# One encoder layer on one core: linear attention's scores in two groups, gate logits and norm sums as high and low parts, two groups of attention values together, and a second queue for the first loads

## The chip, the core and the metric

The kernel runs on one core of a Trainium2 chip. Time is device microseconds of one execution, and the figure for a kernel is the median over several executions. Beside it stands one execution under the hardware profiler, whose span (first to last instruction) and rows are used for all the reasoning. The engines are named as in the profile: PE (matmul) and PEld (its weight loads, which overlap with PE), DVE (VectorE), ACT (ScalarE), POOL (GpSimd) and SP (SyncE, which mostly issues DMAs). ACT and POOL can issue DMAs too.

## The reference

One layer of a hybrid streaming encoder over 512 tokens of width 2048, all in float32. Cut to what matters here:

```python
h = rms_norm(x)
q_a, k_a, v_a, q_g, k_g, v_g, r_g, gate_lr = split(h @ w_in)
# group A: 16 heads of 64, softmax attention over a band of chunks, learned bias by distance
y_a = chunked_band_attention(q_a, k_a, v_a, bias)
# group B: 4 heads (key width 128, value width 256), chunks of 64 tokens
gate_logit = gate_lr @ w_gate_up + b_gate          # rank 16 -> 512
log_a = log_sigmoid(gate_logit) / 16
b = cumsum(log_a within a chunk)
attn = tril((q_g * exp(b)) @ (k_g * exp(-b)).T)    # within a chunk
o_g = attn @ v_g + (q_g * exp(b)) @ S              # S: state carried over the chunks
y_g = rms_norm(o_g, over 256) * silu(r_g)
x = x + concat(y_a, y_g) @ w_out
x = x + (gelu(conv3(up gate)) * conv3(up value)) @ w_ffn_down
x = x + sigmoid(rms_norm(x) @ w_ple_gate) * (p @ w_ple_proj)
return rms_norm(x)
```

## The kernel before

Activations are kept transposed: features on the 128 partitions, the 512 tokens along the free axis. The large products run in fp32r, the faster matmul type, with each fp32 operand split into a high part (a copy rounded to fp32r, made by ACT) and a low part (the difference, made by DVE), and three products high-high, high-low and low-high. `vproj` and `proj` do this for 128x512 tiles. Small products of linear and softmax attention run in plain fp32, which the profile shows as two PE passes each.

The program has three parts.

The start: eleven matmuls of a tile of ones (`pw`, L82) keep PE busy while the first loads travel. All loads go out on SP: the first half of the first value weight, `cols` (all the small per-feature vectors), the first block of `x`, the second half of the weight, and so on (`wtile`, `load_input`). ACT begins with a one-element activation, `warm`, which makes it load its function table.

Linear attention (from about 85 to 317 us in the profile): two value projections `vproj`; the low-rank gate `plr`, whose 32 rows hold the 16 outputs for the high and for the low half of the weight; then for each of four heads `gla_proj` (gate logits `pz` at L1077, exponentials, key and query projections `pk` and `pq`) and `gla_core`. `gla_core` transposes the keys (`pkt`), forms the scores `pat`, the state updates `pu`, the outputs `po`, the sum of squares `s2`, and hands it to `rstd_wide`, whose one fp32 matmul with a matrix of ones (`msw`) spreads the sum over all partitions. `pat` is made of two products for each of four 128-token tiles: a 128x128 one (L1139) and one with 64 output rows for the odd chunk against the even one (L1141). A head's core is issued behind the next head's projections, and two value projections for softmax attention (`values_a`) surround the last core. In this part the order on each engine comes from the scheduler of the tile framework.

The unit machine (from 317 us on): every remaining large product is a "unit" of seven products of 24 matmuls of 128x256 (a two-level block scheme: PLAIN gives their order P1, P2, P6, P5, P7, P3, P4). Units run one after the other as a list of steps, one product a step. From here on `keep_in_program_order` fixes each engine's order as written. Other work is hung on the steps by an agenda: an entry (step, k) runs its function before the product for k up to 1 and behind it for k over 1. The first two steps are `embedding` products `pp`; units 0 to 7 of the front stage are query/key projections, and `attend` hangs the softmax attention of two heads on the steps that follow each. It works in three groups h = 0, 1, 2 of query tiles (TILES): scores, `soft` (bias, maximum, exponential), `normal` (divide by the sum), `turn` (transposes `ptr`), `evict` (ACT copies `ptr` to `PT`) and `values` (`py`, fp32 with 64 output rows, the two heads in the two halves of the PSUM bank). Units 8 to 11 are the output gates of linear attention; then come the output projection `wo`, the feed-forward stages, and the embedding gate.

PSUM: linear attention uses four banks for accumulators (`mm`) and four for small results (`aux`). The unit machine reopens the eight banks as tags b0 to b7, which take their place in the order in which they are first used. Since the first user is `pp`, on the tags b5, b6, b7, b4, these get the banks that hold the last value projection.

Raw weights, high parts and low parts lie in rings of three pages each (`wr`, `wh`, `wl`) in the first two parts; a load into a page waits until the page's former content has been split.

The order of the items in a step, around the change:

```python
(5, 6, scores), (6, 1, soft), (7, 1, normal), (7, 5, turn), (8, 1, evict), (8, 4, values)   # each + h
```

Of the kernel before, what the change touches and what calls it, by code (L numbers as in the profile page):

```python
# [8 lines left out]
F32 = mybir.dt.float32  # L9
F32R = mybir.dt.float32r  # L10
I32 = mybir.dt.int32
AF = mybir.ActivationFunctionType
ALU = mybir.AluOpType

P = 128
# [26 lines left out]
def encoder_block(ctx: ExitStack, tc: tile.TileContext, A, out):  # L42
# [33 lines left out]
    epst = cp.tile([P, 1], F32, name="epst")  # L76
    nc.gpsimd.memset(epst, EPS)
    warm = cp.tile([P, 1], F32, name="warm")
    nc.scalar.activation(warm, ones[:, 0:1], AF.Copy)
    pw = pa.tile([P, T], F32, tag="aux", name="pw")  # L80
    for _ in range(11):
        nc.tensor.matmul(pw[:, :P], ones, ones, start=True, stop=True)  # L82
# [104 lines left out]
        ten.matmul(pb, ones, dg[:, :nt * P], start=True, stop=True)  # L187
        return pb

    def rstd_wide(sumsq, n, dst, a):  # L190
        c = sumsq.shape[1]
        ms = psum_aux("msw")[:, :c]
        ten.matmul(ms, ones, sumsq, start=True, stop=True)
        act.activation(dst, ms, AF.Ln, scale=1.0 / n, bias=epst)
        t = tp.tile([P, T], F32, tag="dg", name="nwt")[:, :c]
        vec.tensor_scalar(a, ms, 1.0 / n, EPS, ALU.mult, ALU.add)
        act.activation(dst, dst, AF.Exp, scale=-0.5)
        vec.tensor_tensor(t, dst, dst, ALU.mult)
        vec.scalar_tensor_tensor(t, t, -0.5, a, ALU.mult, ALU.mult)
        vec.scalar_tensor_tensor(dst, t, 1.5, dst, ALU.add, ALU.mult)  # L200
# [6 lines left out]
    def xslot(i, name):  # L207
        return pairs[i % 8][:, i // 8, :]
# [4 lines left out]
    gnw = cols[:, 4 * KD + 4:4 * KD + 6]  # L213

    h1 = []

    def load_input(kt):
        if kt == 0:
            nc.sync.dma_start(cols, A["cols"])
        xt = xslot(kt, f"x0_{kt}")  # L220
        nc.sync.dma_start(xt, A["x"][kt])
        h = slot(kt, f"h1_{kt}")
        split_scaled(h, xt, nmix[:, kt:kt + 1])
        h1.append(h)
        return xt
# [469 lines left out]
    def attend(unit):  # L695
# [42 lines left out]
                    ten.matmul(psc[:, w], ql, M["Kl", s][:, :nn], start=False, stop=True)  # L738

        def soft(h):  # L740
            t, at = tile_("sc", 1024, bufs=2), 0
            for s in range(2):
                for i, qt in enumerate(TILES[h]):
                    n = P * (qt + 1)
                    sc = M["sc", s, qt] = t[:, at:at + n]
                    mx = M["mx", s, qt] = tile_("mx", 4, bufs=8)
                    at += n
                    vec.tensor_tensor_reduce(sc, M["psc", s, h][:, 256 * i:256 * i + n], bias[:, s, T - n:T], 1.0, -3.0e38,
                                             ALU.add, ALU.max, mx[:, 0:1])
                    vec.tensor_scalar(mx[:, 1:2], mx[:, 0:1], -1.0, None, ALU.mult)  # L750
                    act.activation(sc, sc, AF.Exp, bias=mx[:, 1:2], accum_out=mx[:, 2:3])
# [14 lines left out]

        def evict(h):
            n = 3 * P if h else T
            M["PT"] = tile_("PT", 2 * T).rearrange("p (s t) -> p s t", s=2)
            for s in range(2):  # L770
                act.activation(M["PT"][:, s, :n], M["ptr", s][:, :n], AF.Copy)

        def values(h):
            if h == 0:
                M["y"] = pp_.tile([P, T], F32, tag="b3", name="py")
            for i, qt in enumerate(TILES[h]):
                for kt in range(qt + 1):
                    for s in range(2):
                        o = (2 * i + kt) * P
                        ten.matmul(M["y"][s * 64:(s + 1) * 64, qt * P:(qt + 1) * P], M["V"][:, kt, s * 64:(s + 1) * 64],  # L780
                                   M["PT"][:, s, o:o + P], start=kt == 0, stop=kt == qt)

        def result():
            if b % 2 == 0:
# [5 lines left out]
            items.append((12, 1, lambda: store_pair(mixd, b // 2, ypair[0][:, 0, :], ypair[0][:, 1, :])))  # L790
        for h in range(3):
            items += [(t + h, k, lambda f=f, h=h: f(h)) for t, k, f in (
                (5, 6, scores), (6, 1, soft), (7, 1, normal), (7, 5, turn), (8, 1, evict), (8, 4, values))]
        return items

    tails = [None, None]
# [229 lines left out]
    with ExitStack() as mix:  # L1026
        vp = mix.enter_context(tc.tile_pool(name="v", bufs=1, side="right"))

        with ExitStack() as gctx:
# [20 lines left out]

            for c in range(2):
                vproj(A["w_v_g"], c, lambda t: V[:, t, c * T:(c + 1) * T], c == 0, input_pair if c else None)
            up2 = gp.tile([P, T], F32, name="up2")[0:32]
            nc.sync.dma_start(up2, A["gate_up"])

            gl = page("wr", "wgate_r")
            nc.sync.dma_start(gl[:, :256], A["w_gate"])
# [7 lines left out]
            for kt in range(KD):  # L1065
                w = glh[:, kt * 32:kt * 32 + P]
                nc.tensor.matmul(plr, w, h1[kt][:, 0, :], start=kt == 0, stop=False)
                nc.tensor.matmul(plr, w, h1[kt][:, 1, :], start=False, stop=kt == KD - 1)
            lr = gp.tile([P, T], F32, name="lr")[0:32]
            nc.vector.tensor_tensor(lr, plr[0:32, :], rb[0:32, :], ALU.mult)  # L1070

            def gt(name, tag, bufs=1, cols=T):
                return gp.tile([P, cols], F32, tag=tag, name=name, bufs=bufs)
# [49 lines left out]
            def gla_core(hd, eb, en, dd, dec2):  # L1123
# [13 lines left out]
                for t in range(TT):  # L1137
                    sl = slice(t * P, (t + 1) * P)
                    nc.tensor.matmul(pat[:, sl], en[:, sl], eb[:, sl], start=True, stop=True)  # L1139
                    e0, o0 = t * P, t * P + CHUNK  # L1140
                    nc.tensor.matmul(pat[0:CHUNK, o0:o0 + CHUNK], dd[:, e0:e0 + CHUNK], eb[:, o0:o0 + CHUNK],  # L1141
                                     start=True, stop=True)
# [33 lines left out]
                        nc.vector.tensor_tensor(s2, s2, s3, ALU.add)  # L1176
                    o.append(ov)
                rg = gt("rg", "rg")
                rstd_wide(s2, 256, rg, gt("nwa", "nwa"))
                for vb in range(2):  # L1180
                    nc.vector.scalar_tensor_tensor(o[vb], o[vb], gnw[:, vb:vb + 1], rg, ALU.mult, ALU.mult)
                    nc.sync.dma_start(ond[hd][:, vb], o[vb])
# [40 lines left out]
    values_a(1, operand_step, operands_left)  # L1223
    pctx.close()
    pp_ = ctx.enter_context(tc.tile_pool(name="banks", bufs=1, space=PSUM, reuse_waits="tile"))
    aux[0] = aux_bank
    actx = ExitStack()

# [210 lines left out]
```

## Time and profile before

| what | value |
|---|---|
| time, median of 3 | 2319.01 us (2318.95 to 2320.66) |
| profiled execution | 2315.06 us |
| its span | 2313.4 us |
| mean granted PE clock | 0.995 |
| PE / DVE / ACT / POOL busy | 98% / 81% / 56% / 6% of the span |
| DMA | 516.64 MB, 223 GB/s on average |
| chain that ended last | PE 86%, DVE 6%, DMA 4%, ACT 2%, issue 2% |

In a row of the timeline stand start, duration, engine, line, operation, output and inputs, shapes, count, and in brackets the idle time of the engine just before with what ended it. A matmul's duration is its latency through the array; matmuls overlap, so what one costs is the distance from its start to the next one's start. Where a helper records an instruction, its line is L64.

### The profile page before, as it was taken

The page shows a single profiled execution, that of the slowest core. Times are in us where ns is not written, and L with a number is a line of the kernel's source. Part 1 is how long each engine was busy: PE and PEld are TensorE (multiplying, and loading weights), DVE is VectorE, ACT ScalarE, POOL GpSimd, SP SyncE. Part 2 cuts the span into 40 slices and gives each one's busy share as a digit, 9 for nine tenths or more (in the row PEclk, how much of TensorE's full clock was granted, in tenths as well). Part 3 has the DMA queues.
Part 4 walks back from the last instruction along what each step waited for, and adds up shares of the span by engine and source line. Part 5 has one row for each costly group of instructions (what it writes and reads, how often), then busy time and mean ns, then how long its engine had stood idle before and what let it go on. Part 6 is the DMA issues. An engine that isn't in the chain of part 4 may idle for free.

```text
span 2313.4 us, 44977 instructions
## 1 busy us (share of the span) xinstructions
PE 2272.6 (98%) x18020; PEld 2191.4 (95%) x18020; DVE 1885.2 (81%) x2584; ACT 1295.3 (56%) x1899; POOL 143.0 (6%) x180
## 2 busy tenths in 40 slices
PE   9999999999999999999999999999999999999996
PEld 8878889999989999999999999999999999999996
DVE  6556358888778888998888888888898787898986
ACT  6344356777555665555555555555564554656655
POOL 0000000000000000000000000000000100000000
PEclk9999999999999999999999999999999999999999
DMA  6622586666978977787877777777866967779894
GB/s 219 194 78 87 167 288 170 181 182 186 308 245 265 316 221 206 214 220 209 223 204 219 212 214 207 216 209 219 267 206 228 314 216 251 267 252 330 263 294 164
DMA packets 195473, 516.64 MB, mean 223 GB/s; under 512 B 20896, under 2 KB 72352, under 8 KB 195264
## 3 DMA queue, kind: packets, MB, share of 16 engines
q1 hardware_dynamic: 166272, 422.54, 52.1%
q0 software_dynamic: 23616, 84.95, 20.9%
q10 hardware_dynamic: 5376, 6.29, 0.8%
q8 instruction: 141, 2.31, 0.4%
q14 instruction: 68, 0.56, 0.1%
HBM read 435.05 MB, written 76.55 MB: 221 GB/s over the span
## 4 chain that ended last, share of the span: by engine, by line
PE 86%; DVE 6%; DMA 4%; ACT 2%; issue 2%; ACTq 0%; DVEq 0%; POOL 0%; SPq 0%; POOLq 0%
PE accA L64 39%; PE accC L64 21%; PE accB L64 10%; PE v L249 3%; PE v L250 2%; PE v L251 2%; DVE wl L64 1%; PE py L64 1%; PE psc L64 1%; PE ptr L64 1%; DVE s L64 1%; PE pk L133 1%; PE pk L132 1%; DMA wo_T<-mix_T 1%; PE pk L134 1%
## 5 line engine op out<-in xcount | busy, mean ns | idle before, releaser
L64 DVE TENSOR_TENSOR wl<-s,wh 128x1024 fp32r<-128x1024 f32 (+1 forms) x365 | 437.7, 1200 | 65.2 <-ACT wh L64 64.1
L64 ACT ACTIVATE wh<-l 128x1024 fp32r<-128x1024 f32 (+1 forms) x308 | 319.2, 1037 | 182.8 <-PE accC L64 120.3
L64 DVE TENSOR_TENSOR wl<-l,wh 128x1024 fp32r<-128x1024 f32 (+1 forms) x308 | 368.0, 1195 | 61.9 <-ACT wh L64 61.2
L64 ACT ACTIVATE wh<-s 128x1024 fp32r<-128x1024 f32 (+1 forms) x365 | 377.8, 1036 | 39.2 <-DVE s L64 20.4
L64 ACT ACTIVATE u<-accA 128x256 f32<-128x256 f32 x290 | 109.4, 377 | 363.4 <-PE accA L64 363.2
L64 DVE TENSOR_TENSOR s<-s,l 128x1024 f32<-128x1024 f32 (+1 forms) x192 | 229.6, 1196 | 11.0 <-DMA s<-in_w_blk 10.8
L64 PE MATMUL accA<-up_T,wh 128*128 128x256 f32 x1408 | 178.8, 279 | 0.1
L64 PEld LDWEIGHTS accA<-up_T,wh 128*128 128x128 f32 x1408 | 170.7, 188 | 0.3 <-ACT wh L64 0.3
L64 DVE SCALAR_TENSOR_TENSOR cv<-u,cw,cv 128x511 f32<-128x511 f32 (+1 forms) x176 | 131.6, 748 | 3.1
L404 POOL DMA_DIRECT2D s<-in_w_up x88 | 75.1, 853 | 788.6 <-DMA s<-in_w_up 366.2
L250 PE MATMUL v<-wv_l,h 128*128 128x512 f32 x256 | 100.5, 392 | 0.0
L249 PE MATMUL v<-wv_h,h 128*128 128x512 f32 x256 | 100.3, 392 | 0.0
L251 PE MATMUL v<-wv_h,h 128*128 128x512 f32 x256 | 99.9, 391 | 0.0
L64 PE MATMUL accA<-up_T,wl 128*128 128x256 f32 x704 | 96.4, 279 | 0.0
L64 PE MATMUL accA<-dn_T,wh 128*128 128x256 f32 x704 | 91.6, 282 | 4.5 <-ACT wh L64 4.5
L64 PE MATMUL accB<-up_R,wh 128*128 128x256 f32 x704 | 90.4, 280 | 2.0 <-DVE up_R L64 1.3
L64 PEld LDWEIGHTS accA<-dn_T,wh 128*128 128x128 f32 x704 | 86.8, 190 | 5.1 <-ACT wh L64 5.1
L64 ACT ACTIVATE u<-accC 128x256 f32<-128x256 f32 x94 | 35.9, 382 | 96.2 <-PE accC L64 96.1
L64 PE MATMUL accA<-up_R,wh 128*128 128x256 f32 x704 | 89.7, 280 | 0.0
L64 PE MATMUL accC<-up_R,wh 128*128 128x256 f32 x704 | 89.3, 279 | 0.0
L64 PE MATMUL accC<-up_N,wh 128*128 128x256 f32 x704 | 89.3, 279 | 0.0
L64 PE MATMUL accA<-up_N,wh 128*128 128x256 f32 x704 | 89.3, 279 | 0.0
(383 smaller groups left out, 5124.1 us busy)
## 6 DMA issues: line engine op xcount, KB each, us to landing
l<-in_w_up SPq DMA_DIRECT2D x132, 512.0 KB, 5.5
s<-in_w_up SPq DMA_DIRECT2D x88, 512.0 KB, 4.8
s<-in_w_up POOLq DMA_DIRECT2D x88, 512.0 KB, 6.1
l<-in_w_dn SPq DMA_DIRECT2D x56, 448.0 KB, 5.5
l<-in_w_blk SPq DMA_DIRECT2D x36, 512.0 KB, 4.4
l<-in_w_out SPq DMA_DIRECT2D x28, 512.0 KB, 5.1
l<-in_w_dn SPq DMA_DIRECT2D x28, 512.0 KB, 5.5
s<-in_w_blk SPq DMA_DIRECT2D x24, 512.0 KB, 4.3
```

What stands on the lines that cost most here:

```text
L64: ins = f(*args, **kw)
L132: nc.tensor.matmul(po, whi, act[:, 0, :], start=start, stop=False)
L133: nc.tensor.matmul(po, whi, act[:, 1, :], start=False, stop=False)
L134: nc.tensor.matmul(po, wlo, act[:, 0, :], start=False, stop=stop)
L249: nc.tensor.matmul(ps[t], h1[kt][:, 0, sl], wh, start=kt == 0, stop=False)
L250: nc.tensor.matmul(ps[t], h1[kt][:, 0, sl], wl, start=False, stop=False)
L251: nc.tensor.matmul(ps[t], h1[kt][:, 1, sl], wh, start=False, stop=kt == KD - 1)
L404: nc.gpsimd.dma_start(t, src("L22" if name == "S1" else "L11"), accum_op=ALU.add)
```

## The change

Seven edits.

1. First loads. `x[0]` and then `cols` are issued by ACT, ahead of its table load and `warm`, instead of by SP, so that SP issues the two halves of the first weight back to back.
2. Gate logits. `pz` becomes one fp32r matmul over 128 rows instead of an fp32 one over 32. The gate weight is loaded three times into one raw page and split (`up2`: high, high, low, zero), and the low-rank activations are split alike (`lr`: high, low, high, zero). For that `up_r` takes a page of the ring `wr`, `gate_up` is loaded by three DMAs in place of one, and there are new small operations: one POOL memset, four ACT copies, two DVE subtractions.
3. Norm sums. `s2` is split into `s2h` (ACT) and `s2l` (DVE), and `msw` becomes two fp32r matmuls with a copy of the ones (`ones_r`) instead of one fp32 matmul.
4. Scores of linear attention. The four 128x128 products of `pat` come first, then the four with 64 output rows.
5. Values of softmax attention. `values` of group 1 moves one step later, where `values` of group 2 runs: the twelve matmuls of each head pair stand together. `PT` grows from 1024 to 1536 columns to hold both groups.
6. `sc` becomes one buffer of 1024 columns (groups 0 and 2) and one, `scb`, of 768 (group 1), instead of two of 1024.
7. Four unused tiles are opened first on the tags b0 to b3, so that these take the four former accumulator banks, and b4 to b7 the four former `aux` banks.

The scheduler of the first two parts also shifts neighbours: the first `pz` stands some ten matmuls further down in PE's order, `msw` of each head three further down with its second half behind one more matmul, and in heads 2 and 3 `pz` between the two halves.

```diff
-    nc.scalar.activation(warm, ones[:, 0:1], AF.Copy)
...
-    def rstd_wide(sumsq, n, dst, a):
-        c = sumsq.shape[1]
+    def rstd_wide(ones_r, parts, n, dst, a):
+        c = parts[0].shape[1]
         ms = psum_aux("msw")[:, :c]
-        ten.matmul(ms, ones, sumsq, start=True, stop=True)
+        for i, q in enumerate(parts):
+            ten.matmul(ms, ones_r, q, start=i == 0, stop=i == len(parts) - 1)
...
+    first = xslot(0, "x0_0")
+    nc.scalar.dma_start(first, A["x"][0])
+    nc.scalar.dma_start(cols, A["cols"])
+    nc.scalar.activation(warm, ones[:, 0:1], AF.Copy)
     def load_input(kt):
-        if kt == 0:
-            nc.sync.dma_start(cols, A["cols"])
-        xt = xslot(kt, f"x0_{kt}")
-        nc.sync.dma_start(xt, A["x"][kt])
+        xt = xslot(kt, f"x0_{kt}") if kt else first
+        if kt:
+            nc.sync.dma_start(xt, A["x"][kt])
...
-            t, at = tile_("sc", 1024, bufs=2), 0
+            t, at = (tile_("scb", 768) if h == 1 else tile_("sc", 1024)), 0
...
-            M["PT"] = tile_("PT", 2 * T).rearrange("p (s t) -> p s t", s=2)
+            if h < 2:
+                M["PTt"] = tile_("PT", 3 * T)
+            pt = M["PT", h] = M["PTt"][:, 768 * (h == 2):][:, :2 * n].rearrange("p (s t) -> p s t", s=2)
...
-                (5, 6, scores), (6, 1, soft), (7, 1, normal), (7, 5, turn), (8, 1, evict), (8, 4, values))]
+                (5, 6, scores), (6, 1, soft), (7, 1, normal), (7, 5, turn), (8, 1, evict), (8 + (h == 1), 4, values))]
...
-            up2 = gp.tile([P, T], F32, name="up2")[0:32]
-            nc.sync.dma_start(up2, A["gate_up"])
+            upr = page("wr", "up_r")[:, :T]
+            nc.gpsimd.memset(upr[96:P], 0.0)
+            for i in range(3):
+                nc.sync.dma_start(upr[32 * i:32 * i + 32], A["gate_up"])
+            up2 = gp.tile([P, T], F32R, name="up2")
+            nc.scalar.activation(up2, upr, AF.Copy)
+            nc.vector.tensor_tensor(up2[64:96], upr[64:96], up2[64:96].bitcast(F32), ALU.subtract)
...
-            lr = gp.tile([P, T], F32, name="lr")[0:32]
-            nc.vector.tensor_tensor(lr, plr[0:32, :], rb[0:32, :], ALU.mult)
+            lr = gp.tile([P, T], F32R, name="lr")
+            lf = gp.tile([P, T], F32, tag="lf", name="lrf")[0:32]
+            nc.vector.tensor_tensor(lf, plr[0:32, :], rb[0:32, :], ALU.mult)
+            nc.scalar.activation(lr[0:32], lf, AF.Copy)
+            nc.scalar.activation(lr[64:96], lf, AF.Copy)
+            nc.scalar.activation(lr[96:P], attn_t[0][96:P], AF.Copy)
+            nc.vector.tensor_tensor(lr[32:64], lf, lr[0:32].bitcast(F32), ALU.subtract)
+            ones_r = gp.tile([P, P], F32R, name="ones_r")
+            nc.scalar.activation(ones_r, ones, AF.Copy)
...
                     nc.tensor.matmul(pat[:, sl], en[:, sl], eb[:, sl], start=True, stop=True)
+                for t in range(TT):
                     e0, o0 = t * P, t * P + CHUNK
...
-                rstd_wide(s2, 256, rg, gt("nwa", "nwa"))
+                sh, sl = (gp.tile([P, T], F32R, tag=n, name=n) for n in ("s2h", "s2l"))
+                nc.scalar.activation(sh, s2, AF.Copy)
+                nc.vector.tensor_tensor(sl, s2, sh.bitcast(F32), ALU.subtract)
+                rstd_wide(ones_r, (sh, sl), 256, rg, gt("nwa", "nwa"))
...
     pp_ = ctx.enter_context(tc.tile_pool(name="banks", bufs=1, space=PSUM, reuse_waits="tile"))
+    for t in range(4):
+        pp_.tile([P, T], F32, tag=f"b{t}", name="unused")
```

More of the change, by code (lines that the diff above doesn't have):

```diff
@@ L768, in evict @@
             n = 3 * P if h else T
-            M["PT"] = tile_("PT", 2 * T).rearrange("p (s t) -> p s t", s=2)
+            if h < 2:
+                M["PTt"] = tile_("PT", 3 * T)
+            pt = M["PT", h] = M["PTt"][:, 768 * (h == 2):][:, :2 * n].rearrange("p (s t) -> p s t", s=2)
             for s in range(2):
-                act.activation(M["PT"][:, s, :n], M["ptr", s][:, :n], AF.Copy)
+                act.activation(pt[:, s], M["ptr", s][:, :n], AF.Copy)
         def values(h):
@@ L780, in values @@
                         ten.matmul(M["y"][s * 64:(s + 1) * 64, qt * P:(qt + 1) * P], M["V"][:, kt, s * 64:(s + 1) * 64],
-                                   M["PT"][:, s, o:o + P], start=kt == 0, stop=kt == qt)
+                                   M["PT", h][:, s, o:o + P], start=kt == 0, stop=kt == qt)
         def result():
```

## The prediction

> **What bounds the kernel now.** I read the page first, then windows by stage, then the timeline of PE at every place that the diff touches, then the chain of waits over the passage from the query and key units to the output projection.
>
> ```profile
> PE 2272.6 (98%) x18020; PEld 2191.4 (95%) x18020; DVE 1885.2 (81%) x2584; ACT 1295.3 (56%) x1899; POOL 143.0 (6%) x180
> ...
> PE 86%; DVE 6%; DMA 4%; ACT 2%; issue 2%; ACTq 0%; DVEq 0%; POOL 0%; SPq 0%; POOLq 0%
> ```
>
> ```profile
> 100.00:317.00 217.00, 216.72 (x1014) 174.82 (x1012) 110.81 (x150) 93.80 (x111) 1.97 (x3) 1.00 0.41 131
> ...
> 330.00:553.00 223.00, 222.96 (x1954) 215.05 (x1952) 197.49 (x454) 155.70 (x307) 14.46 (x17) 1.00 0.67 188
> 553.00:620.00 67.00, 64.42 (x536) 61.58 (x535) 47.67 (x90) 38.28 (x60) 4.26 (x5) 0.97 0.82 244
> 620.00:680.00 60.00, 54.50 (x406) 50.94 (x405) 49.73 (x67) 40.49 (x65) 3.40 (x4) 1.00 0.91 297
> ```
>
> The windows give, after the stretch and its length, the busy time of PE, PEld, DVE, ACT and POOL, then PE's granted clock, the DMA engines' share and GB/s. In linear attention (100 to 317) PE is busy for 216.72 of 217 us and DVE for half; in the softmax attention (330 to 553) for 222.96 of 223, with DVE at 89%. So in both a PE slot that is saved brings the end of the stage forward by its length, and work added to ACT or DVE costs nothing while it comes in time. Behind 553 PE does wait, and DMA is busier.
>
> **1. First loads.** Rows of the timeline, weight loads of PE:
>
> ```profile
> 1.20 4.77 PEld L82 LDWEIGHTS pw<-ones 128*128 128x128 f32 x22 [1.20 <-POOL ones L75]
> 6.29 0.29 PEld L249 LDWEIGHTS v<-wv_h,h 128*128 128x128 f32 x1 [0.32 <-ACT h L154]
> ```
>
> The warm-up products keep their number, and their last weight load ends at 5.97; the first real one waits 0.32 us longer, for the first block of `x`. The change issues that block two queue entries earlier, so it should no longer be late, but PE can gain no more than the 0.32. SP's later loads go out earlier too. ACT's table load and `warm` move behind its two DMA issues, in time in which ACT waits for the weight anyway. Below zero: sharing the engines with the first weight half could make that later; I bound it by the same 0.32. I take 0.25 (0.32 to -0.32).
>
> **2 and 3. Gate logits and norm sums.** PE's rows; a cost is the distance between starts.
>
> ```profile
> 159.30 0.40 PE L132 MATMUL pk<-h,wkg_h 128*128 128x512 f32 x1
> 159.55 1.12 PE L64 MATMUL msw<-s,ones 128*128 128x512 f32 x2
> 160.61 1.12 PE L1077 MATMUL pz<-lr,up 32*128 32x512 f32 x2
> ...
> 162.00 0.39 PE L134 MATMUL pk<-h,wkg_l 128*128 128x512 f32 x1
> ```
>
> ```profile
> 222.59 0.40 PE L249 MATMUL v<-wv_h,h 128*128 128x512 f32 x1
> 222.84 1.12 PE L64 MATMUL msw<-s,ones 128*128 128x512 f32 x2
> ...
> 224.04 0.39 PE L251 MATMUL v<-wv_h,h 128*128 128x512 f32 x1
> 224.27 0.39 PE L249 MATMUL v<-wv_h,h 128*128 128x512 f32 x1
> ```
>
> An fp32r product of 128x512 costs 0.23 (224.04 to 224.27). From 222.59 to 224.04 lie two such products and `msw`: 1.45 - 0.46 = 0.99 for `msw`. From 159.30 to 162.00 lie two of them, `msw` and `pz`: 2.70 - 0.46 = 2.24, so `pz` costs 1.25. Four heads: 4 x 2.24 = 8.96. New: one product for `pz`, two for `msw`, 12 x 0.23 = 2.76. Gain 6.2.
>
> What could be late instead:
>
> ```profile
> 158.14 0.63 ACT L1175 ACTIVATE s<-pair_r 128x512 f32<-128x512 f32 x1 [0.71 <-DVE pair_r L1170]
> ```
>
> ```profile
> 158.81 0.69 DVE L1176 TENSOR_TENSOR s<-s,s 128x512 f32<-128x512 f32 x1
> ```
>
> The sum of squares is ready at 159.50. `s2h` on ACT (0.63, as the row of ACT) gives 160.13, `s2l` on DVE (0.69) 160.82. PE's new places are three products behind the old one (159.55 + 0.69 = 160.24), and for the second half two more (160.70). So the first is just in time and the second about 0.1 late. On ACT the logarithm of the norm waits behind `s2h` and the next gate's first activation; PE needs neither soon. I charge 0.1 per head, at worst 0.7 (a whole `s2l`). The first `pz` waits for a longer chain (product, two copies, subtraction), but stands ten products, 2.3 us, further down; that is about its length, so at most one copy, 0.63, is exposed; I take zero. Gain 6.2 - 0.4 = 5.8, between 6.2 and 2.8.
>
> The page for `up_r` and its three DMAs push the gate weight back:
>
> ```profile
> 88.66 0.42 ACT L1062 ACTIVATE glh<-wgate_r 128x256 fp32r<-128x256 f32 x1 [1.43 <-DMA wgate_r<-in_w_gate]
> ```
>
> ```profile
> L1067 PE MATMUL plr<-h,glh x16: 389/394/404, 95.4 to 102.4; 128*128 128x512 f32 x16
> ```
>
> Its split starts at 88.66, is 0.4 us of ACT and as much of DVE, and PE wants it at 95.4. Three issues ahead of it, `up2`'s copy (0.63) and subtraction (0.69) come to under 3 us; the slack is over 5. Nothing. The memset is on an idle POOL, `ones_r` and the zero rows lie in the first 40 us, where PE runs without a wait.
>
> **4. Scores.**
>
> ```profile
> 149.39 0.39 PE L1139 MATMUL pat<-eb,en 128*128 128x128 f32 x2
> 149.71 0.33 PE L1141 MATMUL pat<-eb,dd 128*64 128x64 f32 x2
> 149.97 0.49 PE L1139 MATMUL pat<-eb,en 128*128 128x128 f32 x2
> 150.39 0.33 PE L1141 MATMUL pat<-eb,dd 128*64 128x64 f32 x2
> ...
> 152.00 1.56 PE L1151 MATMUL pu<-Vg,kT 128*128 128x256 f32 x6
> ...
> 154.09 0.61 PE L1166 MATMUL po<-attnT,Vg 128*128 128x128 f32 x4
> 154.53 0.39 PE L1168 MATMUL po<-eb,S 128*128 128x128 f32 x2
> ```
>
> ```profile
> L1141 PEld LDWEIGHTS pat<-eb,dd x32: 132/134/136, 149.7 to 267.3; 128*64 128x64 f32 x32
> ```
>
> Today the eight products take 152.00 - 149.39 = 2.61. Fp32 products of one shape cost 0.22 (154.09 to 154.53 holds two); in `pat` the 128x128 ones cost 0.32 and 0.42, the small ones 0.26, so each change of shape adds 0.1 to 0.2. Grouped: three at 0.22, one at 0.32 before the change, three small ones, one small one at 0.26 before the next shape. If the three small ones cost half of a 128x128 one, 0.11 to 0.13, the sum is 1.6 and a head gains 1.0; if each still costs its 0.26, the sum is 2.02 and a head gains 0.6. I take the first, since half the columns stream: 4 x 1.0 = 3.9 with the roundings, between 4.1 and 2.4. The Trainium skill bears on this (TensorEngine Tiling (Array Packing), Tiling Modes and Restrictions and Gotchas): changing the tiling mode drains the engine, which agrees with the 0.1 to 0.2 above, but column tiling also switches the fast weight load off. The second speaks against my value; it is the third rival.
>
> **5 and 6. Values of two groups.**
>
> ```profile
> 406.13 1.09 PE L64 MATMUL py<-PT,va 128*64 128x128 f32 x16
> 407.16 0.87 PE L64 MATMUL ptr<-ident,sc 128*128 128x128 f32 x6
> ...
> 409.76 1.10 PE L64 MATMUL accA<-in_N,wl 128*128 128x256 f32 x8
> 410.79 0.88 PE L64 MATMUL py<-PT,va 128*64 128x128 f32 x12
> 411.60 0.88 PE L64 MATMUL ptr<-ident,sc 128*128 128x128 f32 x6
> ...
> 417.99 1.10 PE L64 MATMUL accA<-in_T,wl 128*128 128x256 f32 x8
> 418.92 2.03 PE L64 MATMUL accC<-in_R,wh 128*128 128x256 f32 x16
> ```
>
> Eight value products (16 passes) take 1.03, six 0.81: 0.11 each plus 0.15 fixed. Entering costs another 0.10 (409.76 to 410.79 is 1.03, the same eight matmuls before a product of their own shape 0.93). One visit fewer saves 0.25 a unit. The transposes of group 2 move up by 0.81, to the end of their step's product, about 3 us behind the step's start where DVE did the division; in units 0 to 6 PE does not wait there. In unit 7 it does:
>
> ```profile
> 579.52 0.63 PE L64 MATMUL ptr<-ident,sc 128*128 128x128 f32 x3 [0.22 <-DVE mx L64]
> ```
>
> There DVE is the bound, and what PE saves it waits. Seven units: 1.8, bounds 2.2 (unit 7 too) and 0 (each such wait eats the visit). The buffers `sc`, `scb` and `PT` are each rewritten at least as long after their last reader as now: nothing.
>
> **7. Banks.**
>
> ```profile
> 317.77 0.73 PE L64 MATMUL pp<-ps,wh 128*128 128x512 f32 x2 [1.05 <-ACT pair_c L255]
> ```
>
> The first `pp` waits for ACT to evict the last value projection. With `pp` in the former `aux` banks that wait goes, since its inputs were ready before. Late next is the fifth `pp`, which needs the first one's bank; PE comes there at about 322.2 and ACT has emptied it at about 321.9. Gain 1.05, at worst 0.
>
> **The sum.** 0.25 + 5.8 + 3.9 + 1.8 + 1.05 = 12.8, best 13.9, worst 4.9 with all lower ends at once. The profiled execution took 2315.06 us with a span of 2313.4, 4 us less than the median 2319.01. I carry the difference over: span 2300.6, profiled 2302.3, median 2306.
>
> **The rivals.**
>
> First, the passage to the output projection absorbs it. The chain of waits there:
>
> ```profile
> 584.53 10.39 DMA s<-in_w_blk
> ...
> 635.00 14.68 DMA wo_T<-mix_T
> ```
>
> DMA shares of 0.82 and 0.91 speak for it: if the data could not come sooner, PE would arrive 12 us earlier and wait that long. Against it: before, the share is 0.67 with no backlog, and both transfers are issued by work that itself moves up. Up to the point where these waits take all of it, 2319.
>
> Second, slower: the transfers there meet in another order. SP issues in order, so one entry that waits holds all behind it:
>
> ```profile
> SPq L273 <- DVE u L64: 9.2, 1, 9.2
> ```
>
> A gain of 12.8 and 4.6 beyond it are used up by two more holds of this length (18.4) in front of loads that PE needs: 2325. One alone leaves it faster, 2315. It decides from 17.4 us of new waiting. Only the last unit's values end later than now (by 0.65), so little drives it.
>
> Third, weight loads bound the grouped small scores. Their row gives 134 ns, twice per product: 0.27, no less than today's 0.26. Then edit 4 gains 0.6 a head, and the time is 2307.5. The skill's rule on column tiling would do this. Against it: `py` has 16 weight loads of that kind in 1.03, though it alternates between two column halves.
>
> **How the numbers follow.** Forecast 2306, with chance 0.61; third rival 0.17; late operands or small shape gains, 7 to 10 us, 0.10; absorbed 0.06; slower 0.06. Own range of the forecast 2304 to 2308. For 8 in 10 I go from 2302.5 (all best ends, and 2 us of waits in the passage gone) to 2312 (gains near 7). A difference of 0.2%, 4.6 us, is about what a measurement can tell. Faster 0.87 (all but the last two, less a share), same 0.07, slower 0.06.
>
> **What would show it.** `pz` and `msw` as single passes 0.23 apart, without waits on ACT or DVE of more than 0.2; the eight `pat` products in 1.6 us (2.0 for the third rival); `py` x24 once per unit and a unit in 27.3 instead of 27.6; `pp` directly behind the last `v`; the first `v` at about 6.0; the DMA waits in the passage no longer than 10.4 and 14.7 us. The prediction is wrong if PE shows new waits between 100 and 553, or if those two grow.

## The result, and the profile after

The changed kernel takes 2308.41 us (median of 18 runs, 2299.2 to 2315.38), the kernel before 2321.2 us (18 runs, 2310.43 to 2327.45). The ratio is 0.9949, 95% interval 0.9936 to 0.9962: 11.8 us faster, between 8.8 and 14.9. A later comparison gave 0.9931 (0.9905 to 0.9956). Single runs of one kernel lie up to 18 us apart, more than the change is worth; one source of that is shown below. So all parts of the change are read from starts of instructions in the profile, and most of them from several profiles.

The profiled execution of the changed kernel took 2304.32 us, its span 2302.6. From the page, the lines on busy time and on the chain that ended last:

```profile
PE 2261.4 (98%) x18016; PEld 2189.7 (95%) x18016; DVE 1888.0 (82%) x2590; ACT 1300.7 (56%) x1908; POOL 144.0 (6%) x181
...
PE 87%; DVE 6%; DMA 3%; ACT 3%; issue 2%; DVEq 0%; ACTq 0%; POOLq 0%; SPq 0%
```

PE is busy 11.2 us less (2272.6 before), and still bounds the kernel. The same windows as before, of the changed kernel (length of the stretch, then PE, PEld, DVE, ACT, POOL, the granted clock, DMA share, GB/s):

```profile
100.00:317.00 217.00, 216.79 (x1048) 179.55 (x1047) 117.09 (x158) 103.06 (x126) 1.97 (x3) 1.00 0.43 140
330.00:553.00 223.00, 220.99 (x1949) 214.93 (x1947) 194.26 (x454) 153.05 (x302) 15.37 (x18) 0.99 0.70 185
553.00:620.00 67.00, 65.00 (x550) 63.31 (x549) 49.78 (x92) 38.98 (x62) 3.41 (x4) 0.97 0.84 262
620.00:680.00 60.00, 55.01 (x410) 51.47 (x409) 48.82 (x65) 39.07 (x62) 3.41 (x4) 1.00 0.83 272
```

In the first window 34 more matmuls fit into the same 217 us; the busy share hides the gain, since PE is full in both kernels. In the second, PE has 2.0 us of waits that the kernel before did not have. In the two windows behind 553, which hold somewhat later work than before, PE waits 7.0 us instead of 8.1.

Scores, gate logits and norm sums stand like this in the changed kernel's timeline of PE:

```profile
147.70 1.06 PE L1157 MATMUL pat<-eb,en 128*128 128x128 f32 x8
148.68 0.68 PE L1160 MATMUL pat<-eb,dd 128*64 128x64 f32 x8
149.29 1.56 PE L1170 MATMUL pu<-Vg,kT 128*128 128x256 f32 x6
...
157.26 0.39 PE L131 MATMUL pk<-h,wkg_h 128*128 128x512 f32 x1
157.52 0.50 PE L64 MATMUL msw<-s2h,ones_r 128*128 128x512 f32 x1
157.85 0.39 PE L1095 MATMUL pz<-lr,up 128*128 128x512 f32 x1
158.08 0.40 PE L132 MATMUL pk<-h,wkg_h 128*128 128x512 f32 x1
158.32 0.43 PE L64 MATMUL msw<-s2l,ones_r 128*128 128x512 f32 x1
158.58 0.39 PE L133 MATMUL pk<-h,wkg_l 128*128 128x512 f32 x1
```

The eight products of `pat` take 149.29 - 147.70 = 1.59 instead of 2.61. From 157.26 to 158.58 lie two fp32r products of `pk` (0.46) and the three new ones: 0.86 for `msw` and `pz` together, where the kernel before needed 2.24. Three products at 0.23 would be 0.69; the rest is small waits for operands just written (the weight loads wait 0.3 a head for `s2h` and 0.2 for `s2l`).

The table gives, between places that can be found in every profile, the mean over two profiles of the kernel before and three of the changed one (us).

| stretch on PE | before | after | gain | what changed in it |
|---|---|---|---|---|
| start to first `v` | 6.65 | 6.33 | 0.3 | edit 1 |
| first to last `v` | 310.1 | 301.4 | 8.7 | edits 2, 3, 4 |
| last `v` to first `pp` | 1.44 | 0.23 | 1.2 | edit 7 |
| first `pp` to unit 1's `accB` | 34.1 | 35.2 | -1.1 | a new wait for ACT |
| unit 1's to unit 2's `accB` | 23.7 | 25.1 | -1.5 | waits for accumulating loads (DMAs that add what they bring to what lies in the target) |
| unit 2's `accB` to first `wo` product | 271.6 | 268.5 | 3.1 | edit 5, and a shorter passage |

(`accB` is used by one product of a unit, so from one to the next is a unit's period; the softmax attention of unit 0 hangs on unit 1's steps.) The sum, before rounding, is 10.8 us up to the output projection. Behind it nothing was changed.

### The profile page after: what moved, and what is told of

Read it like the earlier page. It is cut to its first block, busy times and chain, and to the rows that moved or that the text cites. A ratio compares the mean times of both kernels' runs of the same rounds, so it can differ in the third digit from the quotient of the medians.

```text
span 2302.6 us, 44996 instructions
## 1 busy us (share of the span) xinstructions
PE 2261.4 (98%) x18016; PEld 2189.7 (95%) x18016; DVE 1888.0 (82%) x2590; ACT 1300.7 (56%) x1908; POOL 144.0 (6%) x181
## 4 chain that ended last, share of the span: by engine, by line
PE 87%; DVE 6%; DMA 3%; ACT 3%; issue 2%; DVEq 0%; ACTq 0%; POOLq 0%; SPq 0%
PE accA L64 40%; PE accC L64 21%; PE accB L64 10%; PE v L252 3%; PE v L254 3%; PE v L253 3%; DVE wl L64 1%; DMA s<-in_w_blk 1%; PE py L64 1%; PE ptr L64 1%; PE psc L64 1%; DVE s L64 1%; DMA s<-in_w_out 1%; DVE u L64 1%; DVE xs L64 1%
## 5 line engine op out<-in xcount | busy, mean ns | idle before, releaser
L64 PEld LDWEIGHTS accB<-up_R,wh 128*128 128x128 f32 x704 | 86.7, 190 | 2.7 <-DVE up_R L64 1.6
```

Of the source, the lines that this page charges most:

```text
L64: ins = f(*args, **kw)
```

## The experiments

### The changed kernel again, and two ways for the first loads

Unedited, under `after_again`:

> The changed kernel a second time, unedited. In its first profile PE's lead over the kernel before fell from 9.6 us (first pp product) to 8.5 at 326 us and to 6.3 at 369 us, the second time behind an accumulating load that landed 7.9 us after its issue. Theory A (a product of the order of work): the same rows fall in the same places, the product waiting for DVE's sc by about 2.0 us. Theory B (variation of the DMA): the fall of 1.1 at 326 stays, since ACT's queue causes it, while the one of 2.7 at 369 is smaller than 1 or absent. All starts before 320 us should agree to 0.1 us with the first profile.

Edit 1 undone, under `e_first_old`:

```diff
+    nc.scalar.activation(warm, ones[:, 0:1], AF.Copy)
...
-    nc.scalar.dma_start(first, A["x"][0])
-    nc.scalar.dma_start(cols, A["cols"])
-    nc.scalar.activation(warm, ones[:, 0:1], AF.Copy)
...
-        xt = xslot(kt, f"x0_{kt}") if kt else first
-        if kt:
-            nc.sync.dma_start(xt, A["x"][kt])
+        if kt == 0:
+            nc.sync.dma_start(cols, A["cols"])
+        xt = xslot(kt, f"x0_{kt}")
+        nc.sync.dma_start(xt, A["x"][kt])
```

> The changed kernel with edit 1 undone (x[0] and cols back on SP between the weight halves, warm first on ACT). Theory: the second queue put the weight halves back to back, so the first half landed later and cols last; without it the first v starts at 6.29 again (6.42 with the edit) and all rows up to 300 us are 0.1 earlier. Rival: the first v is bound by the memory system and not by the queues; it stays at 6.4.

Only `cols` on ACT's queue, under `e_cols`:

```diff
-    nc.scalar.dma_start(first, A["x"][0])
     nc.scalar.dma_start(cols, A["cols"])
...
-        if kt:
-            nc.sync.dma_start(xt, A["x"][kt])
+        nc.sync.dma_start(xt, A["x"][kt])
```

> The changed kernel with only cols on ACT's queue (issued first there), x[0] back on SP between the two weight halves. If the first v waits for cols and x[0] in the order of their issue, x[0] goes out 0.5 us earlier than before and the first v starts at 6.0 to 6.1. If all that counts is the total of bytes ahead of x[0] and the weight half, it starts at 6.25 to 6.35, as before.

Measured: the first `v` starts at 6.31 in `after_again`, 6.71 in `e_first_old`, 5.92 in `e_cols`. So the theory on edit 1, formed from one pair of profiles (6.42 against 6.29), falls: with the old loads the first `v` is not earlier. Nor does it stay at 6.4, as the rival had it. The profiles of all kernels here, sorted by their first loads, show how far one can trust one pair. Old loads: 6.29, 7.01, 5.73, 7.13, 6.71 (mean 6.57). Edit 1: 6.42, 6.31, 6.25, 6.36, 6.74, 6.27 (mean 6.39). Only `cols` on ACT: 5.92, 5.92, 5.58 (mean 5.81). Edit 1 gains 0.2 on average, within a scatter of over 1 us. In the changed kernel ACT waits for `cols` last, behind `x[0]`:

```profile
4.59 0.63 ACT L126 ACTIVATE wv_h<-wv_r 128x512 fp32r<-128x512 f32 x1 [1.35 <-DMA wv_r<-in_w_v_g]
5.65 0.72 ACT L153 ACTIVATE h<-pair_r,cols 128x512 fp32r<-128x512 f32 x1 [0.43 <-DMA cols<-in_cols]
6.42 0.19 PEld L252 LDWEIGHTS v<-wv_h,h 128*128 128x128 f32 x1 [0.44 <-ACT h L153]
```

In the kernel before, the weight half is split at 3.50; here it is at 4.59. It is 3.50 to 3.57 in all five profiles with the old loads, 4.43 to 4.87 in the six with edit 1 and 4.09 to 4.48 in the three with `cols` alone on ACT: the second load travels at the same time. The Trainium skill says (DMA: Bandwidth & Descriptors, Rules for kernel authors) that spreading loads over several issuing engines brings no bandwidth and only saves issue time. The traces agree. With `cols` alone on the second queue the wait for it is gone, and `x[0]` goes out at 1.26 where it went at 1.73 in the kernel before. The first `v` is at 5.9, the earlier of the two values expected, and 0.1 below it. In `e_cols` its weight load waits for nothing but the warm-up products:

```profile
5.85 0.33 PEld L250 LDWEIGHTS v<-wv_h,h 128*128 128x128 f32 x1
```

Those are not fixed either: their last weight load ends at 5.97 in the kernel before, where they lie 0.213 us apart to the end, and at 5.06 in `best_banks`, where the last seven distances are 0.112. The point at which the distance falls differs from profile to profile; what sets it is not shown.

The other part of `after_again`: the wait of 1.1 at 326 us is there again, to 0.01 us. The wait for `sc` is 1.28 instead of 2.02. Neither theory is met in full: the place is reproduced, the size is not. The starts before 320 us agree to 0.24 us and not to 0.1.

### Edit 7 undone, and edit 7 alone

```diff
-    for t in range(4):
-        pp_.tile([P, T], F32, tag=f"b{t}", name="unused")
```

> The changed kernel with edit 7 undone (no unused tiles, so pp takes the banks of the last value projection). Theory: edit 7 moves the first pp up by 1.2 us, but ACT is full between 310 and 329 us and the step behind waits for it, so 1.1 of it is lost at 326 us: without the edit the first pp is 1.0 to 1.2 later (307.0 becomes 308.1 or more on the profile's scale, counted from the last v), and the products behind 330 us start within 0.2 us of the changed kernel's. Rival: the loss at 326 us comes from the other edits, and then the products behind 330 us start 1.0 to 1.2 later.

In the timeline of this kernel the old wait in front of `pp` is back, and the product that waited 1.07 us in the changed kernel waits for nothing:

```profile
308.25 0.39 PE L254 MATMUL v<-wv_h,h 128*128 128x512 f32 x1
309.69 0.72 PE L64 MATMUL pp<-ps,wh 128*128 128x512 f32 x2 [1.05 <-ACT pair_c L258]
...
326.75 2.15 PE L64 MATMUL accA<-in_N,wh 128*128 128x256 f32 x16
```

The same place in the changed kernel:

```profile
308.14 0.63 PE L64 MATMUL pp<-ps,wh 128*128 128x512 f32 x2
...
326.32 2.13 PE L64 MATMUL accA<-in_N,wh 128*128 128x256 f32 x16 [1.07 <-ACT u L64]
```

From the last `v` to that product it is 326.32 - 307.91 = 18.41 with edit 7 and 326.75 - 308.25 = 18.50 without. So the theory stands: of the 1.2 us that edit 7 gains at `pp`, 0.1 is left. ACT's rows say why. Between the splits and copies of that stretch, in order, it has no room, and it empties `accA` late:

```profile
322.10 2.01 ACT L64 ACTIVATE in_R<-in_R 128x1024 fp32r<-128x1024 f32 x2 [0.44 <-ACT pp_o L64]
324.01 1.04 ACT L64 ACTIVATE wh<-s 128x1024 fp32r<-128x1024 f32 x1
324.96 1.04 ACT L64 ACTIVATE in_T<-in_T 128x1024 fp32r<-128x1024 f32 x1
325.91 0.36 ACT L64 ACTIVATE u<-accA 128x256 f32<-128x256 f32 x1
```

This kernel had something else: no wait for `sc` in front of unit 0's first transposes. That made edit 7 a suspect for those waits too, so it was put alone into the kernel before:

> The kernel before with edit 7 alone (four unused tiles on b0 to b3). Theory: the first pp comes 1.2 us earlier, the product behind loses 1.1 of it to ACT, and the accumulating loads of unit 0 now fall behind other transfers: DVE's sum waits 3 us and more for them instead of 1.3, and PE waits 1.3 to 2.4 us for sc in front of unit 0's first ptr. Then the first py starts 1 to 3 us later than before although the first pp is earlier. Rival: those waits come from the linear attention's earlier end or from the variation of the DMA; then the first py starts 0 to 0.3 us earlier than before (378.6) and no PE wait for sc shows in unit 0.

There the first `py` came at 379.76, 1.2 later than before, with a wait of 2.25 us for `sc`, as the theory said. But all profiles, sorted by edit 7, are less clear. DVE works in order, and one of its sums waits for an accumulating load; behind it stands unit 0's softmax. In the changed kernel:

```profile
362.03 1.23 DVE L64 TENSOR_TENSOR s<-s,l 128x1024 f32<-128x1024 f32 x1 [3.75 <-DMA s<-in_w_blk]
366.65 1.25 PE L64 MATMUL ptr<-ident,sc 128*128 128x128 f32 x8 [2.02 <-DVE sc L64]
```

Without edit 7:

```profile
360.56 1.23 DVE L64 TENSOR_TENSOR s<-s,l 128x1024 f32<-128x1024 f32 x1 [1.34 <-DMA s<-in_w_blk]
```

Where this wait of DVE is 1.5 us or less, PE does not wait for `sc` here; where it is 3.4 to 4.4, PE waits 1.3 to 2.9. Unit 1's to unit 2's `accB` takes 23.3 to 25.0 (mean 23.9) in the five profiles without edit 7, and 23.7 to 27.5 (mean 25.9) in the nine with it. DVE's wait is long in seven of the nine with it and in one of the five without (3.46 us in `e_shape`, stretch 25.0), and one and the same kernel, the changed one, has 3.75, 3.44 and 1.51. So the wait varies without any edit. It was more frequent with edit 7, but fourteen profiles are too few to settle whether edit 7 makes it so. If it does, the edit costs more here than the 0.1 that it gains.

### Shapes of the score products

```diff
-nc.tensor.matmul(pat[0:CHUNK, o0:o0 + CHUNK], dd[:, e0:e0 + CHUNK], eb[:, o0:o0 + CHUNK],
+nc.tensor.matmul(pat[:, o0:o0 + CHUNK], dd[:, e0:e0 + P], eb[:, o0:o0 + CHUNK],
```

> The kernel before, alternating order kept, with the small products of pat widened from 64 to 128 output rows (128 weight columns), so that the tile shape no longer changes between them. The upper right part of the scores is left wrong by it. Theory (each change of shape costs 0.1 to 0.2 us): the eight products fall from 2.61 to 1.4 to 1.7 us a head. Rival (the alternation of the operands itself, or the small products' own length, costs the time): they stay above 2.3 us.

Its timeline of PE:

```profile
150.10 0.39 PE L1139 MATMUL pat<-eb,en 128*128 128x128 f32 x2
150.32 0.33 PE L1141 MATMUL pat<-eb,dd 128*128 128x64 f32 x2
150.49 0.44 PE L1139 MATMUL pat<-eb,en 128*128 128x128 f32 x2
150.77 0.33 PE L1141 MATMUL pat<-eb,dd 128*128 128x64 f32 x2
...
151.83 1.51 PE L1151 MATMUL pu<-Vg,kT 128*128 128x256 f32 x6
```

The eight products take 1.73 us instead of 2.61, in the old order: the shape did it, 0.11 a product, though the small products had become wider. What the alternation of sizes itself costs is small: 1.73 against 1.59 for the grouped products, which also have narrower small ones. The end of the range expected was 1.7.

### Gate logits undone

```diff
...
-up2 = gp.tile([P, T], F32R, name="up2")
...
+up2 = gp.tile([P, T], F32, name="up2")[0:32]
+nc.sync.dma_start(up2, A["gate_up"])
...
-lr = gp.tile([P, T], F32R, name="lr")
...
+lr = gp.tile([P, T], F32, name="lr")[0:32]
+nc.vector.tensor_tensor(lr, plr[0:32, :], rb[0:32, :], ALU.mult)
```

> The changed kernel with edit 2 undone (pz in fp32 over 32 rows again, msw as high and low parts). Theory: pz costs 1.25 us again instead of 0.23, but PE then arrives later at the query projections, and the two waits of pq for wqg_l (0.5 each) shrink or go, as DVE's chain behind the norm is what binds there; linear attention (first to last v) is 3.1 to 3.8 us longer than in the changed kernel. Rival: the copies of edit 3 cause those waits; they stay, and the part is 4.0 to 4.3 us longer.

Its timeline of PE at the same head:

```profile
159.25 0.49 PE L64 MATMUL msw<-s2h,ones_r 128*128 128x512 f32 x1
159.67 1.12 PE L1086 MATMUL pz<-lr,up 32*128 32x512 f32 x2
160.72 0.51 PE L64 MATMUL msw<-s2l,ones_r 128*128 128x512 f32 x1
161.06 0.39 PE L132 MATMUL pk<-h,wkg_h 128*128 128x512 f32 x1
```

First to last `v` is 304.9 instead of 301.4: edit 2 alone is worth 3.4 to 3.5, inside the range of the theory, and not the 4.1 that four times 1.02 (1.25 - 0.23) gives. The views of what `pq` waited for, first of this kernel, then of the changed one:

```profile
  DVE wqg_l L127: 0.6, 2
```

```profile
  DVE wqg_l L127: 1.0, 2
```

The waits shrink but do not go, so both sides have a part: PE is earlier by edit 2, and what DVE does ahead of that split got no shorter.

### Three groups at one visit

```diff
+            if h == 0:
+                M["mx"] = tp.tile([P, T], F32, tag="sq", name="mx")
...
-                    mx = M["mx", s, qt] = tile_("mx", 4, bufs=8)
+                    mx = M["mx", s, qt] = M["mx"][:, 32 * s + 8 * qt:32 * s + 8 * qt + 4]
...
-            if h < 2:
-                M["PTt"] = tile_("PT", 3 * T)
-            pt = M["PT", h] = M["PTt"][:, 768 * (h == 2):][:, :2 * n]...
+            pt = tile_(*(("PT0", 1024), ("PT1", 768), ("scb", 768))[h])
+            pt = M["PT", h] = pt[:, :2 * n]...
...
-(8 + (h == 1), 4, values)
+(10 - h, 4, values)
```

> The changed kernel with the values of all three groups at one visit (group 0 two steps later, each group with a PT of its own, the maxima in a page of the norms). Theory: one visit fewer saves what the first merger saved, 0.33 us, so a unit of softmax attention takes 26.9 instead of 27.24 us, 2.3 us over seven units. Rival: group 2's transposes come another step part earlier than DVE has divided, and PE waits for sc; the unit stays at 27.2.

From one unit's `accB` to the next it is 27.57 us in the kernel before, 27.24 in the changed one and 26.93 here, the same in each of six units. Two of the rows, of the changed kernel and of this one:

```profile
424.81 2.03 PE L64 MATMUL accB<-in_R,wh 128*128 128x256 f32 x16
...
452.05 2.03 PE L64 MATMUL accB<-in_R,wh 128*128 128x256 f32 x16
```

```profile
424.72 2.03 PE L64 MATMUL accB<-in_R,wh 128*128 128x256 f32 x16
...
451.65 2.03 PE L64 MATMUL accB<-in_R,wh 128*128 128x256 f32 x16
```

The changed kernel's value products, for the reader to compare with the 1.03 and 0.81 of before:

```profile
400.46 1.09 PE L64 MATMUL py<-PT,va 128*64 128x128 f32 x16
401.49 0.87 PE L64 MATMUL ptr<-ident,scb 128*128 128x128 f32 x6
...
408.59 1.53 PE L64 MATMUL py<-PT,va 128*64 128x128 f32 x24
410.05 2.14 PE L64 MATMUL accA<-in_T,wh 128*128 128x256 f32 x16
```

The two groups take 410.05 - 408.59 = 1.46. Each visit saved is worth 0.31 to 0.33 us a unit; in the six units of steady period it brought no new wait. In unit 7 it did: PE waits 1.64 us for DVE in front of the transposes of group 1, where the changed kernel waits 0.18.

### A combination, and what the timing can tell

`best` is the changed kernel with only `cols` on ACT, without edit 7, and with the three groups at one visit; `best_banks` has edit 7 too; `after_timed` is the changed kernel and `before_again` the kernel before.

> The changed kernel with three alterations: only cols on ACT's queue (x[0] on SP as before), edit 7 undone, and the values of all three groups at one visit. Theory: 0.1 to 0.4 us at the first loads, 2.2 us in softmax attention, and 0 to 2 us in unit 0, if the late accumulating loads there come from edit 7: 2 to 4.5 us faster than the changed kernel on the same chip, 14 to 17 us faster than before (0.9930 to 0.9940). Rival: the waits of the passage take what softmax attention gives, and the time is that of the changed kernel within 1.5 us.

> The same with edit 7 left in. If edit 7 makes the loads of unit 0 late, the stretch from unit 0's second product of the third kind to unit 1's is over 25 us (26.0 was the mean of seven kernels with edit 7, 24.2 of three without), and the time is 1 to 3 us longer than without edit 7. If those waits come from the variation of the DMA, the two kernels agree within 1 us.

> The changed kernel, timed on the same chip beside the two: 11 to 13 us faster than before (0.9944 to 0.9953) if the first comparison holds.

> The kernel before a second time. In the three kernels that share its first loads the first v started between 5.73 and 7.13 us. If this is variation of the DMA, this one lies in the same span, not at 6.29 to 0.1; in unit 0 DVE's second wait for an accumulating load is again 1.3 us if the short wait belongs to this order of work, and 3 us or more if it is variation. Between 1000 and 1600 us accumulating products start either 0.1167 or 0.1178 us apart, as in the other profiles, whatever the kernel.

| kernel | median us (range) | ratio to before, 95% |
|---|---|---|
| before | 2317.73 (2308.87 to 2326.6) | |
| `best` | 2301.23 (2297.68 to 2309.39) | 0.9939 (0.9914 to 0.9964) |
| `best_banks` | 2304.27 (2298.88 to 2305.51) | 0.9942 (0.9919 to 0.9965) |
| `after_timed` | 2302.15 (2297.42 to 2309.13) | 0.9931 (0.9905 to 0.9956) |

The three are faster than before and can't be told apart. By the medians `best` is 0.9 us faster than `after_timed`, less than the 2 to 4.5 of its theory and inside the 1.5 of the rival, and 3.0 faster than `best_banks`; the intervals are too wide to decide on either. The changed kernel itself gained 15.6 us by the medians, more than the 11 to 13 expected. In the profiles `best` begins the output projection first of all (632.1, against 635.3 to 638.6 in three profiles of the changed kernel), but a gain of this size is lost in the scatter of the times. The comparison of `best` and `best_banks` therefore does not settle edit 7 either, though these two profiles speak against it: the stretch behind unit 1's `accB` was 23.3 without and 26.6 with it in these profiles. In `before_again` the first `v` came at 7.01, so that start varies, and DVE's second wait for an accumulating load was 1.21 us, the short one that was expected if it belongs to the order of work.

One source of the scatter can be seen in a stage that the change does not touch. A window in the feed-forward stage, of the changed kernel's first profile:

```profile
1000.00:1200.00 200.00, 200.00 (x1717) 200.00 (x1716) 175.29 (x210) 106.67 (x146) 17.97 (x21) 1.00 0.78 212
```

and of its second (`after_again`):

```profile
1000.00:1200.00 200.00, 200.00 (x1700) 200.00 (x1700) 174.64 (x209) 106.80 (x144) 17.97 (x21) 1.00 0.78 211
```

PE is full in both, at the same granted clock, yet starts 1717 products in 200 us or 1700: one each 0.1167 or 0.1178 us. In the first case the distances repeat as 113, 116, 118, 120 ns, in the second as 116, 118, 119, 119, 116, 119 and the like. The pace holds from the stage's entry to its end, 868 to 869 us against 876. Both kernels have both paces (the kernel before 1717 and 1701, the changed one 1717, 1700 and 1701). What chooses was not found. It is 7 to 8 us of the 18 by which single runs differ.

## Why the prediction was right, point by point

It said 2306.0, between 2302.5 and 2312; the time is 2308.41. The ratio is the better measure, since the time of the kernel before also came out 2.2 us higher with more runs: 2319.01 x 0.9949 = 2307.2. The forecast's mechanism held: in linear attention PE is full, and what is taken from it there reaches the output projection nearly in full. The terms were off in both directions, and one that was in no sum filled part of the gap.

So the total alone proves little. 2308.41 lies 0.4 above the forecast's own range of 2304 to 2308, and nearer to the third rival's 2307.5 than to 2306; only the rows tell the two apart. Of the signs that the prediction named, `pat` in 1.59, `py` x24 once a unit, a unit in 27.24, `pp` directly behind `v` and DMA waits that did not grow came out; `pz` and `msw` start 0.26 to 0.34 apart instead of 0.23, and the first `v` comes at 6.3. And its sign of being wrong, new waits of PE between 100 and 553, came too: 1.0 us of weight loads for `wqg_l`, 1.07 for `u`, and 2.02, 1.28 and none for `sc` in the three profiles. The range, wide enough for gains from 7 us on, held in spite of them. Two of its ends do not follow from its own terms: with unit 7 the values make 8 x 0.25 = 2.0 and not 2.2, and 2319.01 less 13.9 and 2 is 2303.1 and not 2302.5.

- **First loads.** Taken as 0.25; 0.2 to 0.3 in the means, but with a scatter of over 1 us. The bounds of 0.32 on either side were far too narrow, because they took a variable wait, and a variable end of the warm-up products, from one profile. The reason given (SP's queue as the obstacle) was only half of it: with edit 1 the weight half landed later and the wait moved to `cols`.
- **Gate logits and norm sums.** Taken as 5.8. First to last `v` gained 8.7 in all, and `pat` 4.1 of it, so these two gave 4.6. The step that failed is "at worst one copy exposed, I take zero" and the 0.1 a head: the first `pz` lost 0.3 (its start is 0.43 behind its neighbour's and 0.31 ahead of the next one's, where 0.23 is regular), the two halves of `msw` cost 0.63 a head with their waits (0.86 less one product of 0.23) and not 0.46 + 0.1, and DVE's split `wqg_l`, which the prediction did not name, became late in two heads. There the weight load waits 0.5 us, and PE loses 0.35 (two starts 0.47 and 0.34 apart instead of 0.23). Together that is 0.3 + 4 x 0.07 + 2 x 0.35 = 1.3, about the 1.2 that was missing. The split's rows of the timeline, first in the kernel before, then in the changed one:

```profile
171.04 1.21 DVE L128 TENSOR_TENSOR wqg_l<-wqg_r,wqg_h 128x1024 fp32r<-128x1024 f32 x1
```

```profile
170.49 1.22 DVE L127 TENSOR_TENSOR wqg_l<-wqg_r,wqg_h 128x1024 fp32r<-128x1024 f32 x1
```

PE had come some 4 us further ahead by then (2.70 at the outputs `po` and 1.38 at `msw` and `pz`), the split only 0.55. By `e_no_pz`, 3.5 of the 4.6 are edit 2's, so 1.1 is left for edit 3, where 4 x (0.99 - 0.46) less the 0.4 charged made 1.7. Edit 3 was not undone by itself, and the wait for `wqg_l` belongs to both.
- **Scores.** Taken as 3.9, measured 4 x 1.02 = 4.1. The third rival falls: the four small products take 149.29 - 148.68 = 0.61, 0.15 each, though their 64 output rows are a tiling of the columns. That the shape's change is what cost the time is shown by `e_shape`. The page of the Trainium skill cited beside the rival lists what column tiling switches off; another page of the Trainium skill (TensorE: Matmul & The Clock Gate, Weight-path perf modes) says that the fast weight load is off for fp32 inputs anyway, so for these products there was nothing to lose. The traces agree as far as they go: the small products start 0.15 us apart, not the rival's 0.27, while their weight load takes 138 ns, as before (134).
- **Values.** Taken as 0.25 a unit, measured 0.33, in six units of steady period. The item behind a visit was left out: six transposes take 0.63 behind value products, and 0.57 where the visit has gone (405.04 to 405.61 in the changed kernel). For unit 7 the prediction said that what PE saves there it waits, and so it came, with a wait that the kernel before does not have in front of that transpose:

```profile
571.04 0.63 PE L64 MATMUL ptr<-ident,sc 128*128 128x128 f32 x3 [1.58 <-DVE mx L64]
```

- **Banks.** Taken as 1.05, "at worst 0"; it is 0.1. Named as late next was the fifth `pp`, which lost only 0.1. What is late is the third product behind the `pp`, through ACT, which the prediction had not followed past `pp`: `u` out of `accA` stands in order behind a row of splits and copies.
- **Unit 0.** Not in the sum: 1.5 us lost on average in the three profiles, by waits for accumulating loads which vary (1.51 to 3.75 on DVE).
- **The passage.** The first rival (it absorbs the gain) falls. The stretch to the output projection became 3.1 us shorter, of which edit 5 is some 2.0 at 0.33 us a unit. The other 1.1 is the passage's, and what brought it is not shown. In the kernel before, PE waited there once more, in the timeline:

```profile
600.01 3.34 PE L64 MATMUL accA<-in_N,wh 128*128 128x256 f32 x16 [1.44 <-ACT u L64]
```

This wait is missing in two of three profiles of the changed kernel and 0.97 in the third. But from the last unit's `accB` to the first `wo` product it is 77.5 to 77.6 in all three; in the kernel before it is 79.2 and 78.0, and 77.5 with edit 7 alone, where the wait was 1.46. So this wait does not explain it, and 1.1 is no more than the kernel before differs from itself there. The prediction had put "2 us of waits in the passage gone" into its lower bound only. Nor does the chain of waits tell the kernels apart. In the changed kernel's first profile it shows at this place:

```profile
620.11 8.68 DMA wo_T<-mix_T
628.86 13.08 DMA s<-in_w_out
```

The second profile of the kernel before shows the same two (8.80 and 12.60), and the second of the changed kernel the old two, with 10.32 for `s<-in_w_blk` and 14.54 for `wo_T<-mix_T`. The second rival (SP's queue holds two more loads) did not occur: SP's hold of 9.2 us in front of `mix_R` is there once in both kernels.

So the forecast of 12.8 met 10.8 to 11.8: 1.2 too much for gate logits and norm sums, 1.0 for the banks and 1.5 lost in unit 0, against 1.1 more in the passage and 0.2 each in the scores and values.

## What to carry to other kernels

When a full engine gets ahead of its helpers, go down the order of each helper (here ACT's copies behind `pp`, DVE's split behind the norm) to the first item that PE needs, past the edited place: one of seven terms was given back there, and another in part. Products of one tile shape belong together: each change cost 0.1 us, and each visit saved 0.3. And before a microsecond is read out of two profiles, profile the same kernel twice: the first loads and the accumulating loads vary by more than most terms here, and so do the waits on the chain, while the length of linear attention, from first to last `v`, repeats to 0.2 us in the nine profiles in which it is the same work (301.36 to 301.56).

## What was not expected

A full PE ran the same stage at two steady paces, 0.1167 and 0.1178 us a product of 128x256, at a granted clock of 1.00 in both; that is 7 to 8 us of 2300, two thirds of what the whole change gained. And the start of the first real product varied from 5.73 to 7.13 us with identical loads.
